# Attention weights of the last 16 keys of each query block: four small transposes and products, and one of each

## The chip, the cores and the metric

The kernel runs on one NeuronCore of a Trainium2 chip. The metric is the device time of one execution in microseconds (us); lower is better. The times given are medians of several runs, with the range.

## The reference

A decoder block on 16 learned meta tokens and 512 tokens (528 rows, model width 1024), all in float32:

```python
h = layer_norm(concat(meta, x))
q_d, k_d, v_d, g_d, q_s, k_s, v_s, g_s, m_d, m_s = split(h @ w_in)        # 1024 x 10240
# 8 differential heads: two softmax maps with a distance bias, their difference times V
a = softmax(q0 @ k0.T / 8 - slope * dist) - lam * softmax(q1 @ k1.T / 8 - slope * dist)
y_d = rms_norm(a @ v) * (1 - lam_init)
# 16 stick-breaking heads
a = exp(log_sigmoid(z) + suffix_sum(log_sigmoid(-z)))      # z = q @ k.T / 8, strictly earlier keys
y_s = a @ v
y = (sigmoid(m_d) * ((y_d * silu(g_d)) @ w_br_d) + sigmoid(m_s) * ((y_s * silu(g_s)) @ w_br_s)) @ w_out
out = layer_norm(2 ** 0.25 * h + y)[16:]
```

Queries are taken in blocks of 128. The meta tokens stand in front, so block i (0 to 3) of queries sees 16 + 128 (i + 1) keys: 144, 272, 400 and 528. Counted in key tiles of 128, block i has full tiles 0 to i and, in tile i + 1, a *strip* of 16 keys. Row r of the block sees strip key k only where r >= 112 + k, so the strip's weights are zero for all but the last 16 queries of the block.

## The kernel before

The work goes by 16 units: 8 differential heads, then 8 pairs of stick-breaking heads. While a unit's attention runs, the projections of the next units (queries, keys, values, gates) fill TensorE; after the last unit come the branch products, the output product and the last norm. Every float32 product that needs accuracy is made of float32r products: a matrix is rounded to a high part (by ScalarE, a cast) and the rest is its low part (by VectorE, a subtraction), and two or three of the four cross products are summed in PSUM. Some small products run in plain float32.

For each head:

- `d_scores` (L817) or `s_scores` (L897) go through the blocks from 3 down to 0. They write the weights of block i to columns `AOFF[i]` on of a padded tile, `apad0` or `apad1`, queries on the partitions. The pad behind the last key of each block is cleared once at the start (L588).
- `transposed` (L762) turns the weights so that keys stand on the partitions. `full` turns a 128 x 128 tile, `strip` the 128 columns that begin with block i's strip. Three steps, each with one PSUM bank (tag `tp`, two buffers): `part0` turns key tile 0 of four blocks into t0; `part1` turns into t1 the strip of block 0, the strip of block 3, and key tile 1 of blocks 1 to 3; `part2` turns into t2 the strip of block 1, key tile 2 of blocks 2 and 3, the strip of block 2, and key tile 3 of block 3. That is 14 transposes. A strip's transpose uses `turned`, an identity turned by 32 columns, so that the block's last 32 queries come out first; the next full tile overwrites the others. So each key tile j has the 32 queries before its first full block and then its full blocks: 512, 416, 288, 160 and 32 columns for tiles 0 to 4 (`QOFF`, L41).
- `split` (L772) makes the high and low parts of each tile (L775 on ScalarE, L776 on VectorE). In a differential head tile 3 (160 columns) is only copied and stays float32 (L808). Tile 4, 16 keys by 32 queries, gets small casts and a subtraction of its own (L793 to L796).
- `values` (L721) turns the V of the unit at hand, projected one unit earlier: four full tiles into tv, and the last 16 keys into t4 (L730, output of 16 partitions), with high and low parts.
- `d_values` (L856) and `s_values` (L918) accumulate V times weights in one bank `av`. A differential head takes tile 0 three times (L861, L869, L870), tile 3 in float32 (L862), tile 4 with high and low parts stacked on the partitions (L863), and tiles 1 and 2 three times each (L866 to L868). A stick-breaking head takes tile 0 twice (L923, L929), tile 4 once (L924) and tiles 1 to 3 twice each (L927, L928).

What sets the order: `run` (L571) gives each step (a block's scores, a part of the transposes, the value products) a place by an estimated time within the unit, and the parts of the projections advance in between. From the units on, a scheduler with a model of each engine then orders the instructions; up to that point and after the attention part, `keep_order` (L233) fixes the order as written. Each engine runs its queue in order, so an instruction that waits holds up all behind it.

Of the kernel before, what the change touches and what calls it, by code (L numbers as in the profile page):

```python
# [16 lines left out]
P = 128  # L17
# [11 lines left out]
AOFF = [0, 256, 640, 1152]  # L29
AW = 1792  # L30
# [10 lines left out]
QOFF = [0, 96, 224, 352, 480]  # L41
# [4 lines left out]
def hybrid_block_kernel(ctx: ExitStack, tc: tile.TileContext, x, meta, emb_g, emb_b, w_in, b_gate,  # L46
# [224 lines left out]
    idents = const.tile([P, 192], F32, name="idents")  # L271
    ident, turned = idents[:, 32:32 + P], idents[:, :P]
    make_identity(nc, ident)
    g.tensor_copy(idents[:, :32], ident[:, 96:])
# [308 lines left out]
    with tc.tile_pool(name="att", bufs=1) as ap:  # L583
        apads = []
        for n in range(2):
            a = ap.tile([P, AW], F32, name=f"apad{n}")
            for i in range(NB):
                g.memset(a[:, AOFF[i] + NKEY[i]:(AOFF + [AW])[i + 1]], 0.0)  # L588
            apads.append(a)

        tails = {}
        v4d = ap.tile([P, P], F32R, name="v4d")
        v4s = ap.tile([P, 4, 64], F32R, name="v4s")
        for n in ("d", 0, 1):
            tails[n] = (v4d if n == "d" else v4s[:, 2 * n:2 * n + 2].rearrange("p c d -> p (c d)"),
                        ap.tile([P, 32], F32R, name=f"a4{n}"))
        for t in (v4d, v4s, *(tails[n][1] for n in tails)):
            g.memset(t.bitcast(F32), 0.0)
# [122 lines left out]
        def values(unit, kind):  # L721
# [7 lines left out]
            t4 = ptp.tile([P, 512], F32, tag="tp", name="t4")[:M, :P]  # L729
            pe.transpose(t4, vT[:, 512:528], ident)  # L730
            if kind == "d":
# [4 lines left out]
                vf = ap.tile([P, P], F32, tag="vf", name="vf")  # L736
                s.copy(vf, tvv[:, 3, :])
                v4 = tails["d"][0]
                s.copy(v4[:M], t4)
                s.copy(v4[32:32 + M], t4)  # L740
                v.tensor_tensor(v4[64:64 + M], t4, v4[:M].bitcast(F32), op=ALU.subtract)
                unit["V"] = V, vf
            else:

                V = V.rearrange("p (j c d) -> p j c d", j=4, c=4)
                for h, l, src in ((V[:, :, 0:4:3], V[:, :, 1:3], tvv.rearrange("p j (c d) -> p j c d", c=2)),
                                  (v4s[:M, 0:4:3], v4s[:M, 1:3], t4.rearrange("p (c d) -> p c d", c=2))):
                    s.copy(h, src)
                    v.tensor_tensor(l, src, h.bitcast(F32), op=ALU.subtract)
                s.copy(v4s[32:32 + M, 0:4:3], t4.rearrange("p (c d) -> p c d", c=2))  # L750
# [11 lines left out]
        def transposed(ta, a, head):  # L762
# [3 lines left out]

            def strip(t, o, i, rot=True):

                c = AOFF[i] + (i + 1) * P
                pe.transpose(t[:, ds(o if rot else o - 96, P)], a[:, c:c + P], turned if rot else ident)  # L770
# [8 lines left out]
            def part0():  # L779
                t0 = ptp.tile([P, 512], F32, tag="tp", name="t0")  # L780
                for i in range(4):
                    full(t0, i * P, i, 0)
                ta[0] = split(t0, 512, 0)

            def part1():
                t1 = ptp.tile([P, 512], F32, tag="tp", name="t1")
                strip(t1, 0, 0)
                strip(t1, 416, 3, rot=False)
                for i in range(1, 4):
                    full(t1, 32 + (i - 1) * P, i, 1)  # L790
                ta[1] = split(t1, 416, 1)
                a4, t4 = tails[head][1], t1[:M, 416:448]
                s.copy(a4[:M], t4)  # L793
                if head == "d":
                    s.copy(a4[64:64 + M], t4)
                v.tensor_tensor(a4[32:32 + M], t4, a4[:M].bitcast(F32), op=ALU.subtract)  # L796
# [462 lines left out]
```

## Time and profile before

| | |
|---|---|
| time, median of 3 runs | 721.54 us (720.97 to 724.15) |
| span of the profiled execution, first to last instruction | 717.8 us |
| granted TensorE clock, mean over the span | 0.996 |
| instructions | 13500 |
| matmul records on TensorE | 4558 |

No total time is given for the profiled execution apart from its span; the median of the runs is 3.7 us above the span, for what lies around it.

In the rows below, PE is TensorE's matmuls, PEld its weight loads, DVE VectorE, ACT ScalarE, POOL GpSimd, SP the DMA-issuing engine. `L765` is a line of the kernel; `t<-idents,apad` says what is written and read, by tile name without buffer number; `128*128 128x416` is a matmul's array size and its moving operand. `x4` is a count. What stands in brackets is the engine's idle time before an instruction and who ended it. Matmul records overlap, so a record's length is longer than the step from its start to the next start. A plain float32 product leaves two records.

### The profile page before, as it was taken

Reading aid. Unit: us, or ns where it says so; the run is one execution under the profiler, and the core shown is the slowest. Engines: PE = TensorE matmul, PEld = TensorE weight load, DVE = VectorE, ACT = ScalarE, POOL = GpSimd, SP = SyncE. Lnnn points to the kernel's source line nnn. Section 1 sums busy time; section 2 is a strip of 40 time slices with the busy share of each in tenths; the row PEclk is TensorE's granted clock in tenths of the full one; section 3 lists DMA queues with packets and bytes.
Section 4 is the critical chain, followed back from the end, with each engine's and each line's share of the span. In section 5 each row is a group of like instructions: output and inputs, shape, how many; then the busy total and the mean of one; then the engine's idle time right before and its main releaser. Section 6 shows DMA issues by size and latency. Waiting matters only on the chain.

```text
span 717.8 us, 13500 instructions
## 1 busy us (share of the span) xinstructions
PE 705.1 (98%) x4558; PEld 643.9 (90%) x4558; DVE 572.1 (80%) x1255; ACT 433.2 (60%) x1041; POOL 126.4 (18%) x151
## 2 busy tenths in 40 slices
PE   8999999999999999999999999999999999999994
PEld 8999999989999888998989899988888998999884
DVE  6887888878696767989887898976396888688887
ACT  5775676757576677867757586765265456555300
POOL 3213210212212111212123020000012102130002
PEclk9999999999999999999999999999999999999998
DMA  9358864779889885998897976556449847696902
GB/s 292 90 168 162 178 143 107 174 164 190 214 173 198 194 179 153 178 230 178 215 215 168 211 157 192 146 151 192 158 121 184 152 120 180 136 187 185 322 17 102
DMA packets 182183, 123.38 MB, mean 172 GB/s; under 512 B 9009, under 2 KB 165074, under 8 KB 182114
## 3 DMA queue, kind: packets, MB, share of 16 engines
q1 hardware_dynamic: 148130, 102.32, 49.5%
q0 software_dynamic: 33664, 19.14, 21.3%
q10 hardware_dynamic: 320, 1.06, 0.4%
q8 instruction: 36, 0.59, 0.3%
q14 instruction: 33, 0.27, 0.1%
HBM read 91.96 MB, written 9.44 MB: 141 GB/s over the span
## 4 chain that ended last, share of the span: by engine, by line
PE 86%; DVE 5%; DMA 3%; ACT 3%; issue 1%; POOL 1%; SPq 0%; ACTq 0%; DVEq 0%; POOLq 0%
PE q L693 15%; PE ps L496 12%; PE ps L497 12%; PE ps L498 12%; PE q L1066 10%; PE ps L512 7%; PE sc L759 6%; PE t L765 4%; PE t L770 1%; DMA lgb<-in_ln_b_dram 1%; PE av L927 1%; PE bank L387 1%; PE tv L726 1%; PE av L928 1%; DVE hr L1216 1%
## 5 line engine op out<-in xcount | busy, mean ns | idle before, releaser
L188 DVE TENSOR_TENSOR wl<-raw,wh 128x512 fp32r<-128x512 f32 x169 | 114.7, 686 | 45.4 <-ACT wh L183 39.1
L497 PE MATMUL ps<-hTl,wh 128*128 128x512 f32 x368 | 144.7, 393 | 0.0
L498 PE MATMUL ps<-hTh,wl 128*128 128x512 f32 x368 | 144.5, 393 | 0.0
L496 PE MATMUL ps<-hTh,wh 128*128 128x512 f32 x368 | 144.5, 393 | 0.0
L183 ACT CAST wh<-raw 128x512 fp32r<-128x512 f32 x169 | 103.0, 620 | 35.3 <-PE ps L497 23.0
L498 PEld LDWEIGHTS ps<-hTh,wl 128*128 128x128 f32 x368 | 69.2, 188 | 13.6
L496 PEld LDWEIGHTS ps<-hTh,wh 128*128 128x128 f32 x368 | 69.2, 188 | 13.3 <-DVE kvt L710 0.3
L497 PEld LDWEIGHTS ps<-hTl,wh 128*128 128x128 f32 x368 | 69.2, 188 | 13.1
L146 POOL DMA_DIRECT2D rawk<-in_w_in_dram x44 | 60.9, 1669 | 95.8 <-DMA rawk<-in_w_in_dram 40.8
L759 PE MATMUL sc<-k,A 128*128 128x264 f32 (+3 forms) x320 | 67.8, 300 | 0.2 <-POOL k L605 0.2
L1066 PE MATMUL q<-gh,wh 128*128 128x256 f32 x224 | 63.5, 283 | 0.2 <-ACT t L1075 0.2
L1066 PE MATMUL q<-gh,wl 128*128 128x256 f32 x224 | 63.4, 283 | 0.0
L1066 PE MATMUL q<-gl,wh 128*128 128x256 f32 x224 | 63.4, 283 | 0.0
L776 DVE TENSOR_TENSOR al<-t,ah 128x512 fp32r<-128x512 f32 (+2 forms) x88 | 45.5, 524 | 20.6 <-ACT ah L775 17.8
L913 DVE TENSOR_TENSOR_SCAN e<-e,diag 128x528 f32<-128x528 f32 (+1 forms) x64 | 53.8, 845 | 7.1 <-ACT e L907 7.1
L775 ACT CAST ah<-t 128x288 fp32r<-128x288 f32 (+3 forms) x88 | 39.8, 462 | 30.1 <-PE t L765 19.8
L759 PEld LDWEIGHTS sc<-k,A 128*128 128x128 f32 x320 | 50.6, 189 | 3.2 <-POOL k L605 0.4
L693 PE MATMUL q<-tS,wh 128*128 128x264 f32 x176 | 50.8, 290 | 0.0
L693 PE MATMUL q<-tl,wh 128*128 128x264 f32 x176 | 50.3, 286 | 0.0
L693 PE MATMUL q<-tS,wl 128*128 128x264 f32 x176 | 50.0, 285 | 0.0
L938 POOL DMA_DIRECT2D ys<-half x14 | 11.8, 840 | 197.0 <-ACT ys L937 187.2
L512 PE MATMUL ps<-hTh,wh 128*128 128x264 f32 x160 | 46.1, 288 | 0.0
(290 smaller groups left out, 1870.5 us busy)
## 6 DMA issues: line engine op xcount, KB each, us to landing
raw<-in_w_in_dram SPq DMA_DIRECT2D x141, 256.0 KB, 3.5
rawk<-in_w_in_dram POOLq DMA_DIRECT2D x44, 256.0 KB, 5.9
rawk<-in_w_in_dram SPq DMA_DIRECT2D x33, 256.0 KB, 4.7
k<-ks SPq DMA_DIRECT2D x60, 132.0 KB, 3.2
raw<-in_w_out_dram SPq DMA_DIRECT2D x16, 256.0 KB, 3.3
k<-ks SPq DMA_DIRECT2D x60, 66.0 KB, 3.2
A<-low SPq DMA_DIRECT2D x28, 128.0 KB, 3.9
raw<-in_w_br_diff_dram SPq DMA_DIRECT2D x12, 256.0 KB, 3.1
```

The source lines that it names most:

```text
L146: second[l] = [lambda raw=raw, x=x: g.dma_start(raw, x, accum_op=ALU.add) for x in more]
L183: s.copy(wh, raw)
L188: eng.tensor_tensor(wl, raw, wh.bitcast(F32), op=ALU.subtract)
L496: pe.matmul(ps, wh[:, k % 4, :], hTh[:, k, M:], start=(k == 0), stop=False)
L497: pe.matmul(ps, wh[:, k % 4, :], hTl[:, k, M:], start=False, stop=False)
L498: pe.matmul(ps, wl[:, k % 4, :], hTh[:, k, M:], start=False, stop=(k == KT - 1))
L512: pe.matmul(ps[:, :H2], a[:, k % 4, :], b[:, k, ts(c, H2)], start=(k == 0 and m == 0), stop=(k == KT - 1 and m == 2))
L693: pe.matmul(bank, a[:, k, :], b, start=start and k == 0 and j == 0, stop=k == 3 and j == 2, skip_group_check=not start)
L759: pe.matmul(ps[:, :n], q, K[:, m, k0:k0 + n], start=(m == 0), stop=(m == 1))
L776: v.tensor_tensor(l, t[:, o:o + w], h.bitcast(F32), op=ALU.subtract)
L913: v.tensor_tensor_scan(rev, rev, diag[0][:, L - nk:][:, ::-1], 0.0, ALU.mult, ALU.max)
L1066: pe.matmul(bank, a[:, k, :], b[:, n, k, :], start=start and k == 0 and m == 0, stop=k == 3 and m == 2, skip_group_check=not start)
```

## The change

The strip of 16 keys is no longer part of the key tiles. Key tiles begin at the block's own first query (512, 384, 256 and 128 columns), and tile 3 stays float32 in both kinds of head.

The four strips of a head are handled together. `strips` lets ScalarE copy them, each twice, into a tile `sx` of 128 columns, ordered (block, copy, key). One transpose gives 4 x 2 x 16 partitions by 128 queries. Only its last 32 queries are used: VectorE repeats them four times along the columns and multiplies by a constant mask `own_block`, which leaves each block's own rows in its own 32 columns (`x`). ScalarE and VectorE then make one float32r tile `m` whose first copies hold the high parts and second copies the low parts, with the sign column `sides`. The product of V's strips, arranged in the same 128 rows, with `m` is written to the last 32 queries of each block, four pieces of 32 columns of `av`. V's 16-key strips (key tiles 128 on, 16 keys each) pass through the same `strips` copy and one transpose of 128 columns.

The padding of the weights' tiles and its clearing go, `idents` becomes a plain identity, and the strips of a head have a common step of 544 columns in the padded tile.

```diff
-AOFF = [0, 256, 640, 1152]
-AW = 1792
+AOFF = [0, 416, 832, 1248]
+AW = 1776
+STRIP, SW = P, 544
...
+        v4 = ap.tile([P, 4, 64], F32R, name="v4")
+        v3 = ap.tile([P, 3, 64], F32, name="v3")
+        own_block = ap.tile([P, NB, 32], F32, name="own_block")
+        sides = ap.tile([P, 2], F32, name="sides")
+        g.memset(own_block, 0.0)
+        for i in range(NB):
+            g.memset(own_block[ds(32 * i, 32), i, :], 1.0)
...
 def values
-            t4 = ptp.tile([P, 512], F32, tag="tp", name="t4")[:M, :P]
-            pe.transpose(t4, vT[:, 512:528], ident)
+            t4 = ptp.tile([P, 512], F32, tag="tp", name="t4")[:, :P]
+            pe.transpose(t4, strips(vT[:, P:], P), ident)
...
+        def strips(t, w):
+            o = ap.tile([P, P], F32, tag="sx", name="sx")
+            s.copy(o.rearrange("p (a h r) -> p a h r", a=NB, h=2), bass.AP(t.tensor, t.offset, [t.ap[0], [w, NB], [0, 2], [1, M]]))
+            return o
...
 def part0
+                ta["strips"] = strips(a[:, STRIP:], SW)
...
 def part1
-                strip(t1, 0, 0)
-                strip(t1, 416, 3, rot=False)
+                pe.transpose(t1[:, 384:], ta["strips"], ident)
                 for i in range(1, 4):
-                    full(t1, 32 + (i - 1) * P, i, 1)
-                ta[1] = split(t1, 416, 1)
-                a4, t4 = tails[head][1], t1[:M, 416:448]
-                s.copy(a4[:M], t4)
-                if head == "d":
-                    s.copy(a4[64:64 + M], t4)
-                v.tensor_tensor(a4[32:32 + M], t4, a4[:M].bitcast(F32), op=ALU.subtract)
+                    full(t1, (i - 1) * P, i, 1)
+                x = ap.tile([P, NB, 32], F32, tag="ax", name="ax")
+                v.tensor_tensor(x, t1[:, 480:].unsqueeze(1).to_broadcast([P, NB, 32]), own_block, op=ALU.mult)
+                m = ap.tile([P, NB, 32], F32R, tag="am", name="am")
+                s.activation(m, x, AF.Identity, scale=sides[:, 1:2])
+                ta[1] = split(t1, 384, 1)
+                v.scalar_tensor_tensor(m, x, sides[:, 0:1], m.bitcast(F32), op0=ALU.mult, op1=ALU.subtract)
+                ta["strips"] = m
...
 def part2
-                strip(t2, 0, 1)
                 for i in range(2, 4):
-                    full(t2, 32 + (i - 2) * P, i, 2)
-                strip(t2, 288, 2)
-                full(t2, 320, 3, 3)
-                ta[2] = split(t2, 288, 2)
-                if head == "d":
-                    ta[3] = ap.tile([P, 160], F32, tag="ah3", name="af3")
-                    s.copy(ta[3], t2[:, 288:448])
-                else:
-                    ta[3] = split(t2, 160, 3, 288)
+                    full(t2, (i - 2) * P, i, 2)
+                full(t2, 2 * P, 3, 3)
+                ta[2] = split(t2, 256, 2)
+                ta[3] = ap.tile([P, P], F32, tag="af3", name="af3")
+                s.copy(ta[3], t2[:, 256:384])
...
 def d_values
-            pe.matmul(av[:, QOFF[3]:], vf, ta[3], start=False, stop=False)
-            pe.matmul(av[:, QOFF[4]:], v4, a4, start=False, stop=False)
+            pe.matmul(av[:, 3 * P:], v3[:, 0:2].rearrange("p c d -> p (c d)"), ta[3], start=False, stop=False)
+            ends = av.rearrange("p (i q) -> p i q", i=NB)[:, :, 96:]
+            pe.matmul(ends, h, ta["strips"], start=False, stop=False)
+            pe.matmul(ends, l, ta["strips"], start=False, stop=False)
...
 def s_values
-            pe.matmul(av[:, QOFF[4]:], v4, a4, start=False, stop=False)
-            for j in range(1, 4):
-                o = av[:, QOFF[j]:]
+            pe.matmul(av[:, 3 * P:], v3[:, c:c + 2].rearrange("p c d -> p (c d)"), ta[3], start=False, stop=False)
+            pe.matmul(av.rearrange("p (i q) -> p i q", i=NB)[:, :, 96:],
+                      v4[:, 2 * c:2 * c + 2].rearrange("p c d -> p (c d)"), ta["strips"], start=False, stop=False)
+            for j in range(1, 3):
+                o = av[:, j * P:]
```

Where instructions moved, at three places of the differential heads. TensorE's transposes of a differential head's weights, into t0 and t1 (the two numbered `t`), between the projection's products; before:

```order
L759 MATMUL sc<-k_456,A_1309 128x264 x4
L512 MATMUL ps<-hTh,wh 128x264
L512 MATMUL ps<-hTl,wh 128x264
L765 MATMUL t_1583<-idents,apad_434 128x128 x4
L770 MATMUL t_1595<-idents,apad_434 128x128 x2
L765 MATMUL t_1595<-idents,apad_434 128x128 x3
L512 MATMUL ps<-hTh,wl 128x264
```

and of the change, whose lines are numbered by its own file:

```order
L510 MATMUL ps<-hTl,wh 128x264
L510 MATMUL ps<-hTh,wl 128x264
L766 MATMUL t_1581<-ident,apad_433 128x128 x4
L784 MATMUL t_1593<-ident,sx 128x128
L766 MATMUL t_1593<-ident,apad_433 128x128 x3
L510 MATMUL ps<-hTh,wh 128x264
```

Nine transposes become eight, and the fifth, of `sx`, reads what ScalarE has copied. In the first head TensorE's value products stand as follows before (`af` is tile 3, `a4d` tile 4, `ah` and `al` the high and low parts):

```order
L862 MATMUL av<-af_927,vf 128x160
L863 MATMUL av<-a4d,v4d 128x32
L866 MATMUL av<-ah_907,V 128x416
L867 MATMUL av<-al_908,V 128x416
L868 MATMUL av<-ah_907,V 128x416
L866 MATMUL av<-ah_923,V 128x288
L867 MATMUL av<-al_924,V 128x288
L868 MATMUL av<-ah_923,V 128x288
```

and with the change (`am` is the block-diagonal tile `m`, `v` the tiles `v3` and `v4`):

```order
L854 MATMUL av<-af_920,v_436 128x128
L856 MATMUL av<-am,v_435 128x4x32
L857 MATMUL av<-am,v_435 128x4x32
L860 MATMUL av<-ah_904,V 128x384
L861 MATMUL av<-al_905,V 128x384
L862 MATMUL av<-ah_904,V 128x384
L860 MATMUL av<-ah_916,V 128x256
L861 MATMUL av<-al_917,V 128x256
L862 MATMUL av<-ah_916,V 128x256
```

The place in the row is the same, one product is added and all others are narrower. ScalarE's queue in the same head, from the last softmax of block 0 to tile 1's cast; before:

```order
L846 ACTIVATE e_455,zs<-e_455,mn 128x144
L183 CAST wh<-raw 128x512
L614 ACTIVATE A_968<-ps 128x512
L846 ACTIVATE e_454,zs<-e_454,mn 128x528
L775 CAST ah_894<-t_889 128x512
L775 CAST ah_907<-t_901 128x416
```

and with the change:

```order
L838 ACTIVATE e_447,zs<-e_447,mn 128x144
L183 CAST wh<-raw 128x512
L760 COPY sx<-apad_433 128x128
L183 CAST wh<-raw 128x512
L611 ACTIVATE A_962<-ps 128x512
L838 ACTIVATE e_446,zs<-e_446,mn 128x528
L771 CAST ah_888<-t_883 128x512
L760 COPY sx<-vT 128x128
L790 ACTIVATE am<-ax,sides 128x128
L771 CAST ah_904<-t_895 128x384
```

The weights' strip copy stands behind one weight cast, V's strip copy and the sign pass between the casts of tiles 0 and 1. On VectorE the mask stands ahead of tile 0's subtraction and the combination behind it.

More of the change, by code (lines that the diff above doesn't have):

```diff
@@ L856, in d_values @@
         def d_values(unit, ta):
-            (vh, vl), vf = unit["V"]
-            v4, a4 = tails["d"]
+            vh, vl = unit["V"]
+            h, l = [v4[:, 2 * m:2 * m + 2].rearrange("p c d -> p (c d)") for m in range(2)]
             av = pav.tile([P, 512], F32, tag="av", name="av")
```

54 lines of the change are left out of this document (19 added, 35 removed).

## The prediction

> **What bounds the kernel now.** I read the page first, then the two long stretches by window, then TensorE's own timeline. The page's busy row, and its row on the chain that ended last by engine:
>
> ```profile
> PE 705.1 (98%) x4558; PEld 643.9 (90%) x4558; DVE 572.1 (80%) x1255; ACT 433.2 (60%) x1041; POOL 126.4 (18%) x151
> PE 86%; DVE 5%; DMA 3%; ACT 3%; issue 1%; POOL 1%; SPq 0%; ACTq 0%; DVEq 0%; POOLq 0%
> ```
>
> TensorE is busy nearly always and carries 86% of the chain. The edit lies in the attention part. Busy times there by window (width, then PE, weight loads, VectorE, ScalarE, GpSimd with counts, granted clock, DMA share, GB/s), the first for the eight differential heads, the second for the eight stick-breaking pairs:
>
> ```profile
> 33.00:251.00 218.00, 217.82 (x1492) 203.44 (x1491) 174.50 (x506) 144.68 (x371) 48.51 (x48) 1.00 0.77 173
> 251.00:522.00 271.00, 270.81 (x1697) 243.43 (x1697) 213.30 (x398) 180.97 (x456) 38.53 (x36) 1.00 0.75 181
> ```
>
> In 489 us TensorE has no record running for 0.18 + 0.19 = 0.37 us, at clock 1.00. VectorE is at 80% and 79%, ScalarE at 66% and 67%, DMA at 0.77 and 0.75: all have room on average. So here the time is the sum of what TensorE is given to do.
>
> Records overlap, since one starts before its forerunner has ended; a duration is not what an instruction costs. I go by the distance from start to start. [...]
>
> **Prices of what goes and comes.** First transposes, and their neighbours, in the first head (timeline of TensorE: start, length of the merged records, count):
>
> ```profile
> 61.80 0.60 PE L765 MATMUL t<-idents,apad 128*128 128x128 f32 x4
> 62.24 0.38 PE L770 MATMUL t<-idents,apad 128*128 128x128 f32 x2
> 62.46 0.49 PE L765 MATMUL t<-idents,apad 128*128 128x128 f32 x3
> 62.70 0.37 PE L512 MATMUL ps<-hTh,wl 128*128 128x264 f32 x1
> 62.91 0.29 PE L512 MATMUL ps<-hTh,wh 128*128 128x264 f32 x1
> ```
>
> From 61.80 to 62.91 nine transposes and one 264-column product start. The chain of waits in order of time has long unbroken runs that price that product, the 256-column one and float32:
>
> ```profile
> 12.45 2.62 PE bank L387 x16
> 15.94 3.51 PE bank L387 x24
> 137.53 1.70 PE q L693 x14
> 550.14 40.31 PE q L1066 x336
> ```
>
> 264 columns: 1.70 / 14 = 0.12 us; 256 columns: 40.31 / 336 = 0.12 us. So a transpose costs (1.11 - 0.12) / 9 = **0.11 us**. L387 multiplies in float32, which leaves two records for each product. Its 16 records are eight of 128 and eight of 256 columns, the 24 are the same and eight more of 128: (3.51 - 2.62) / 8 = 0.111 us a record, **0.22 us** for a 128-column float32 product. Now the value products, stick-breaking then differential:
>
> ```profile
> 279.14 0.34 PE L759 MATMUL sc<-k,A 128*128 128x144 f32 x2
> 279.31 0.23 PE L924 MATMUL av<-a,v4s 128*128 128x32 f32 x1
> 279.39 0.43 PE L927 MATMUL av<-ah,V 128*128 128x416 f32 x1
> 279.66 0.35 PE L928 MATMUL av<-al,V 128*128 128x416 f32 x1
> 279.85 0.29 PE L927 MATMUL av<-ah,V 128*128 128x288 f32 x1
> 279.98 0.40 PE L498 MATMUL ps<-hTh,wl 128*128 128x512 f32 x1
> 280.21 0.39 PE L496 MATMUL ps<-hTh,wh 128*128 128x512 f32 x1
> ...
> 281.14 0.24 PE L928 MATMUL av<-al,V 128*128 128x160 f32 x1
> 281.21 0.43 PE L929 MATMUL av<-al,V 128*128 128x512 f32 x1
> 281.48 0.40 PE L496 MATMUL ps<-hTh,wh 128*128 128x512 f32 x1
> ```
>
> ```profile
> 71.55 0.44 PE L862 MATMUL av<-af,vf 128*128 128x160 f32 x2
> 71.71 0.29 PE L863 MATMUL av<-a4d,v4d 128*128 128x32 f32 x1
> 71.85 0.44 PE L866 MATMUL av<-ah,V 128*128 128x416 f32 x1
> 72.12 0.35 PE L867 MATMUL av<-al,V 128*128 128x416 f32 x1
> 72.31 0.35 PE L868 MATMUL av<-ah,V 128*128 128x416 f32 x1
> ```
>
> 416 columns: 279.85 - 279.66 = 0.19. 288: 0.13. 512: 0.23. From 279.14 to 279.66 stand two products of 144, one of 32 and one of 416: (0.52 - 0.19) / 3 = 0.11 each, so 32 columns cost what 144 do. 160 columns with the 512 behind: 0.34 - 0.23 = 0.11. In the differential head 71.55 to 72.31 holds the float32 product of 160, the 32 and two of 416: 0.76 - 0.38 - 0.11 = 0.27 for the float32 one.
>
> **The change on TensorE, counted over the whole order.**
> - Transposes of weights: 336 become 240 of full tiles and 24 of strips: 72 fewer x 0.11 = **-7.9**. The 16 of V's last keys stay 16.
> - Float32r products of 160 columns in the stick-breaking heads: 32 x 0.11 = **-3.5**.
> - Float32 products: 8 x 0.27 go, 24 x 0.22 come: -2.2 + 5.3 = **+3.1**.
> - Strip products: 24 of 32 columns go (24 x 0.11), 32 of 4x32 columns come (two in a differential head, one in the others): -2.6 + 3.5 = **+0.9**.
> - Narrower tiles: 56 products of 416 become 384. 384 has no row; between 264 (0.12) and 416 (0.19) it is about 0.175: 56 x 0.015 = -0.8. 56 of 288 become 256: 56 x 0.01 = -0.6. **-1.4**.
>
> The unknown is the 4x32 product, 128 float32r columns written in four pieces. The nearest rows, 32, 144 and 160 columns, all give 0.11, which I take; 0.22, the float32 price, is the upper end, +3.5 us in all. Below 0.11 I see no row: even 32 columns take that.
>
> V's strip transpose now loads 128 weight columns where it loaded 16:
>
> ```profile
> L730 PEld LDWEIGHTS t<-idents,vT x10: 87/88/88, 44.8 to 454.4; 128*16 128x16 f32 x10
> 73.36 0.27 PE L730 MATMUL t<-idents,vT 128*16 128x128 f32 x1
> 73.39 0.75 PE L759 MATMUL sc<-k,A 128*128 128x272 f32 x4
> 73.97 0.28 PE L512 MATMUL ps<-hTh,wh 128*128 128x264 f32 x1
> ```
>
> 0.61 us hold it and four products of 272 (about 0.12 each): 0.12 already, so I count nothing. [...]
>
> **The start.** Before the first scores GpSimd clears pads and strip tiles, then K; TensorE waits for it once:
>
> ```profile
> 31.07 1.12 POOL L588 MEMSET apad<- 128x112 f32 x8 [13.76 <-DVE nlam L450]
> 33.42 0.39 PE L759 MATMUL sc<-k,A 128*128 128x264 f32 x1 [0.17 <-POOL k L605]
> ```
>
> The eight pad clears go, five clears of the mask and one ramp for the bias (moved ahead of K) come: K is cleared no later. **-0.2**.
>
> **The other engines, and the added waits.** Rows on single pieces of work (views by tile: least / median / most ns; then one row of VectorE's timeline and one of ScalarE's):
>
> ```profile
> L776 DVE TENSOR_TENSOR al<-t,ah x88: 296/570/693, 63.3 to 515.5; 128x512 fp32r<-128x512 f32 x24, 128x416 fp32r<-128x416 f32 x24, 128x288 fp32r<-128x288 f32 x24, 128x160 fp32r<-128x160 f32 x16
> L796 DVE TENSOR_TENSOR a<-t,a x16: 179/180/181, 276.9 to 511.7; 16x32 fp32r<-16x32 f32 x16
> L793 ACT CAST a<-t x16: 157/172/177, 275.4 to 510.8; 16x32 fp32r<-16x32 f32 x16
> L737 ACT COPY vf<-tv x8: 243/256/262, 47.4 to 232.8; 128x128 f32<-128x128 f32 x8
> 58.91 0.37 DVE L853 SCALAR_TENSOR_TENSOR apad<-e,rz,e 128x144 f32<-128x144 f32 x1
> 59.59 0.62 ACT L183 CAST wh<-raw 128x512 fp32r<-128x512 f32 x1 [1.72 <-PE ps L497]
> ```
>
> VectorE gets 24 masks and 24 combinations of 128 columns, at most 0.37 each (the 144-column row): +17.8; it loses 16 x 0.30 and 24 x 0.18: -9.1. At most +9 on 387.8 us busy. ScalarE gets 40 strip copies and 24 sign passes near 0.26: +16.6, and loses 32 casts of 0.17 and 16 of 160 columns (0.30, taken as VectorE's): +6 on 325.7; V's own casts come out even. Both fit into the idle rest, so they count nothing as long as nobody waits.
>
> Three waits are new. (1) ScalarE copies the strips once VectorE has written the last block; behind it on ScalarE stand a weight cast, the query cast and t0's cast. TensorE turns the strips right behind t0's four transposes; behind it stand three transposes and the projection. The last block ends at 58.91 + 0.37 = 59.28, the strip transposes started at 62.24: 2.96 us, in which ScalarE has one weight cast (to 60.21, after a wait for TensorE) ahead of a copy of 0.26. The copy of V's strip waits for nothing late, since V is a unit old. (2) ScalarE's sign pass waits for VectorE's mask, with the 384-column cast queued behind. (3) VectorE's combination waits for the sign pass, with score work queued behind; the strip product needs it microseconds later. From below these cost nothing; from above one cast of 0.62 in each of 24 heads, 14.9 us. Since the cover is 2.96 against 0.26, I take the low end: as much idle time again as TensorE has now, **+0.4**.
>
> **Sum:** -7.9 - 3.5 + 3.1 + 0.9 - 1.4 - 0.2 + 0.4 = **-8.6 us**, from a span of 717.8 to 709.2. The median of the runs is 721.54, 3.7 us above the span for what lies around it, which stays: **712.9 us**.
>
> **The rivals.**
> - *The 4x32 product costs the float32 price*, for its few columns or its four pieces: +3.5, 716.4. The 144- and 160-column rows speak against it; that no row writes in pieces speaks for it. Chance 0.09.
> - *VectorE becomes the bound* among the stick-breaking heads: it stands still for a cast in progress and the sign pass (0.62 + 0.26) in each of 24 heads, 21 us, of which a quarter reaches TensorE through late weights: +5, about 718. Against it: 57.7 us idle in that window. Chance 0.09.
> - *The weights' DMAs set the pace* and the gain stays as idle time: 717 to 719. DMA shares of 0.77 and 0.75 speak against it. Chance 0.04.
> - *Slower:* TensorE waits at the strip transpose for ScalarE's copy, stuck behind a weight cast that itself waits for TensorE (1.72 us in the row above). It decides from 9.0 / 24 = 0.38 us a head, where the gain is gone; at 0.53 it is slower by 0.5%. A wait of 0.62 + 0.26 a head costs 21.1: 733.6. It needs the 2.96 us of cover to vanish. Chance 0.04.
> - *Forecast:* 0.74.
>
> A measurement of this kernel tells some 0.5%, 3.6 us, from no change. Below 717.9 lie the forecast, the first rival and nearly half of the second: 0.87; within 0.5%: 0.09; slower: 0.04. The forecast's own spread is 710.8 (narrow products cheaper, no hand-off lost) to 715; with the 4x32 price it reaches 716.4, and 717.0 leaves about 0.2 out.
>
> **What would show it.** Right: a TensorE row of 280 transposes, nine starts of L766 and L784 still 0.11 us apart, 4x32 products 0.11 from start to start, TensorE idle under 1 us in the attention windows, which get shorter by about 9 us together, and nothing changed after them. Wrong: TensorE rows with ScalarE's strip copy or VectorE's combination as releaser, 4x32 starts 0.22 apart, or VectorE above 90% in the second window.

## The result, and the profile after

The changed kernel takes **716.64 us** (median of 6 runs, 715.86 to 717.36) where the kernel before, run beside it, takes 721.72 (720.97 to 724.15): a ratio of **0.9928 [0.9905, 0.9951]**, or -5.1 us. The forecast was 712.9, with a range of 710.8 to 717.0. The span of the profiled execution went from 717.8 to 714.6 us, -3.2 where the sum said -8.6. The span missed its forecast by 5.4 us and the time by 3.7 only, because the prediction added too much around the span. Its 3.7 us is the median of the kernel before less the span of its profiled execution, and these are two different executions. Where time and span of one execution are both on record, 1.7 to 2.9 us lie between them, and 1.8 in most (2.4 in the profiled run here). With 1.8 the forecast would have been 711.0. Three single executions of 985 to 4008 us, far above all others of their kernels, are left out of the figures below.

The page's busy row and its row on the chain by engine, and two stretches by window (width; busy time and count of PE, weight loads, VectorE, ScalarE, GpSimd; granted clock; DMA share; GB/s), all of the changed kernel:

```profile
PE 698.9 (98%) x4494; PEld 637.0 (89%) x4494; DVE 571.8 (80%) x1265; ACT 439.1 (61%) x1065; POOL 125.9 (18%) x143
PE 83%; DVE 8%; DMA 4%; ACT 3%; issue 1%; POOL 1%; SPq 0%; DVEq 0%; ACTq 0%; POOLq 0%
33.00:251.00 218.00, 217.78 (x1495) 203.65 (x1495) 177.02 (x516) 148.04 (x379) 49.48 (x49) 1.00 0.78 176
251.00:522.00 271.00, 269.33 (x1655) 240.64 (x1653) 213.15 (x404) 185.34 (x474) 37.26 (x34) 1.00 0.74 178
```

TensorE's share of the chain fell from 86 to 83% and VectorE's rose from 5 to 8%. In the first window TensorE idles 0.22 us, as before. In the second it idles 271.00 - 269.33 = 1.67 us where it idled 0.19. The largest waits of TensorE by who ended them (total us, times, longest):

```profile
PE ps L494 <- ACT wh L183: 1.8, 1, 1.8
PE q L690 <- DVE low L612: 0.9, 2, 0.6
```

The first is one single wait, at the end of the attention part. TensorE's timeline there (start, length, line, out<-in; idle time and its releaser in brackets), for the last head's value products and what follows:

```profile
510.10 0.48 PE L916 MATMUL av<-ah,V 128*128 128x512 f32 x1
...
515.91 0.39 PE L917 MATMUL av<-af,v 128*128 128x128 f32 x2
516.05 0.31 PE L918 MATMUL av<-am,v 128*128 128x128 f32 x1
...
516.43 0.34 PE L923 MATMUL av<-al,V 128*128 128x384 f32 x1
...
516.83 0.39 PE L924 MATMUL av<-al,V 128*128 128x512 f32 x1
...
520.96 0.39 PE L496 MATMUL ps<-hTh,wl 128*128 128x512 f32 x1
523.17 0.64 PE L494 MATMUL ps<-hTh,wh 128*128 128x512 f32 x1 [1.82 <-ACT wh L183]
523.61 0.63 PE L495 MATMUL ps<-hTl,wh 128*128 128x512 f32 x1
524.04 0.69 PE L496 MATMUL ps<-hTh,wl 128*128 128x512 f32 x1
```

From 520.96 to 523.17 are 2.21 us where a step takes 0.23: **1.98 us** stand still. After the restart the steps are 0.43 to 0.44 instead of 0.23. The windows say why (same columns as above; the second number is the width, the number behind the five engines is the granted clock):

```profile
523.00:524.00 1.00, 0.83 (x2) 0.41 (x3) 1.00 (x3) 1.00 (x3) 0.00 (x0) 0.68 0.00 0
524.00:525.00 1.00, 1.00 (x4) 0.81 (x4) 0.72 (x2) 1.00 (x4) 0.00 (x0) 0.50 0.02 6
525.00:526.00 1.00, 1.00 (x4) 0.81 (x3) 1.00 (x3) 0.55 (x2) 0.00 (x0) 0.50 0.68 197
526.00:527.00 1.00, 1.00 (x5) 0.76 (x4) 0.93 (x4) 0.00 (x0) 0.00 (x0) 0.61 1.04 312
```

The granted clock is halved behind the wait: 0.32 + 0.50 + 0.50 + 0.39 = **1.7 us** of TensorE's time are lost. Before, no such stretch stands here:

```profile
523.00:530.00 7.00, 7.00 (x32) 5.82 (x31) 6.40 (x13) 4.59 (x8) 0.00 (x0) 1.00 0.23 68
```

What TensorE waits for is a weight cast at the end of a chain that the last value product starts. ScalarE's and VectorE's timelines of the changed kernel, the links of the chain:

```profile
517.32 0.58 ACT L928 COPY half<-av 64x512 f32<-64x512 f32 x1 [5.75 <-PE av L924]
518.70 0.93 ACT L1043 CAST gh<-ydT 128x256 fp32r<-128x256 f32 x2 [0.81 <-DVE ysT L930]
520.98 1.04 ACT L1043 CAST gh<-t 128x1024 fp32r<-128x1024 f32 x1 [1.34 <-DVE t L1040]
521.93 0.68 ACT L565 ACTIVATE td<-ps,cols 128x512 f32<-128x512 f32 x1
522.51 1.12 ACT L183 CAST wh<-raw 128x512 fp32r<-128x512 f32 x2
```

```profile
517.93 0.69 DVE L930 TENSOR_TENSOR ysT<-av,half 64x512 f32<-64x512 f32 x1 [6.66 <-ACT half L928]
```

From the start of the last value product to TensorE's restart: 523.17 - 516.83 = 6.34 us. TensorE has 18 projection products to fill it, 18 x 0.23 = 4.1 us. In the kernel before, TensorE's and ScalarE's timelines have the same chain:

```profile
515.62 0.43 PE L927 MATMUL av<-ah,V 128*128 128x416 f32 x1
...
518.61 0.30 PE L927 MATMUL av<-ah,V 128*128 128x288 f32 x1
...
519.99 0.43 PE L929 MATMUL av<-al,V 128*128 128x512 f32 x1
```

```profile
520.51 0.58 ACT L933 COPY half<-av 64x512 f32<-64x512 f32 x1 [5.07 <-PE av L929]
525.71 1.13 ACT L183 CAST wh<-raw 128x512 fp32r<-128x512 f32 x2
```

There the cast starts 5.72 us behind the last value product, with the changed kernel 5.68: the chain is as long as ever. What changed is the **cover**. TensorE's order shows it: 947 products of the projections and branches stand behind the last value product before, 930 with the change. The first one that needs the cast is the same, so 35 products cover the chain before (8.0 us) and 18 after (4.1 us).

Why the last value product stands further back is seen in the rows above. The kernel before starts tile 1's products at 515.62 and strews the others between projection products. With the change the float32 product of tile 3 (L917) stands right behind tile 0's in the program, and the scheduler puts it, and so all that follow it, 24 projection products behind tile 0's; then seven come in one block. The copy `af` that it reads had ended at 511.57, over 4 us before:

```profile
511.30 0.27 ACT L802 COPY af<-t 128x128 f32<-128x128 f32 x1 [0.49 <-DVE al L772]
```

So on the chip nothing waits at L917; the lateness is in the order.

The rest of the loss is small. TensorE waits twice for VectorE's `low` of a gate (rows below of the timeline; the step of a 512-column product is 0.23, here 440.37 - 439.26 = 1.11, so 0.88 too long):

```profile
439.26 0.48 PE L916 MATMUL av<-ah,V 128*128 128x512 f32 x1
440.37 0.39 PE L690 MATMUL q<-tS,wh 128*128 128x264 f32 x1 [0.63 <-DVE low L612]
```

Counted from the score products ahead of them, so that the transposes between are included, the places near 314 and 440 us cost 0.6 and 1.1 us; before, one at 261 us cost 0.6. Against the sum of -8.6: +2.0 for the wait, +1.7 for the clock, +1.1 for the small waits, +0.2 for the start, where nothing was gained (before, TensorE waited 0.17 us for the cleared K, now 0.2 for ScalarE's `k`): 5.0 us. The span is off by 5.4, or by 5.8 where the +0.4 for hand-offs that the sum already holds is set against these waits; the rest stays open.

### The profile page after: what moved, and what is told of

It is laid out like the page before. It is cut to its first block, busy times and chain, and to the rows that moved or that the text cites. A ratio compares the mean times of both kernels' runs of the same rounds, so it can differ in the third digit from the quotient of the medians.

```text
span 714.6 us, 13390 instructions
## 1 busy us (share of the span) xinstructions
PE 698.9 (98%) x4494; PEld 637.0 (89%) x4494; DVE 571.8 (80%) x1265; ACT 439.1 (61%) x1065; POOL 125.9 (18%) x143
## 4 chain that ended last, share of the span: by engine, by line
PE 83%; DVE 8%; DMA 4%; ACT 3%; issue 1%; POOL 1%; SPq 0%; DVEq 0%; ACTq 0%; POOLq 0%
PE q L690 15%; PE ps L494 11%; PE ps L495 11%; PE ps L496 11%; PE q L1062 10%; PE ps L510 7%; PE sc L754 5%; PE t L766 3%; PE bank L385 1%; PE tv L723 1%; DMA raw<-in_w_in_dram 1%; DMA raw<-in_w_out_dram 1%; DMA lgb<-in_ln_g_dram 1%; DVE hr L1212 1%; DMA xt<-in_x_dram 1%
## 5 line engine op out<-in xcount | busy, mean ns | idle before, releaser
L772 DVE TENSOR_TENSOR al<-t,ah 128x512 fp32r<-128x512 f32 (+2 forms) x72 | 39.7, 552 | 12.5 <-ACT ah L771 8.6
L771 ACT CAST ah<-t 128x512 fp32r<-128x512 f32 (+2 forms) x72 | 34.2, 477 | 21.3 <-PE t L766 21.1
```

Source lines behind the costliest of these rows:

```text
L772: v.tensor_tensor(l, t[:, o:o + w], h.bitcast(F32), op=ALU.subtract)
```

## The experiments

The **theory**: TensorE's work shrank as predicted (-8.8), and what is missing was lost by the place of tile 3's product: late value products, a chain without cover, a wait, a halved clock. The **rivals**: some product or transpose is dearer than predicted; the new hand-offs on ScalarE and VectorE cost the time; the late cast alone is at fault, wherever the products stand; the profile's wait is an accident. The kernels ran in three sets, each on a chip of its own with the kernel before beside it.

### First set (kernel before: 719.92 us)

**Tile 3 moved behind tiles 1 and 2, all else as changed.**

```diff
 def s_values
             pe.matmul(av, V[c][:, 0, :], ta[0][0], start=True, stop=False)
-            pe.matmul(av[:, 3 * P:], v3[:, c:c + 2].rearrange("p c d -> p (c d)"), ta[3], start=False, stop=False)
...
                 pe.matmul(o, V[c][:, j, :], ta[j][1], start=False, stop=False)
+            pe.matmul(av[:, 3 * P:], v3[:, c:c + 2].rearrange("p c d -> p (c d)"), ta[3], start=False, stop=False)
             pe.matmul(av, V[c][:, 0, :], ta[0][1], start=False, stop=True)
```

> The changed kernel with one line moved: in the stick-breaking heads the float32 product of key tile 3 stands behind the products of tiles 1 and 2 instead of right behind tile 0. Theory A (tile 3, whose weights are ready last, heads the row, so that all seven value products of the last head come late, ScalarE's weight cast behind them comes late, TensorE waits 1.98 us at 523.17 and its clock then falls to half for 3.4 us, 1.9 us more lost): 26 more projection products stand behind the last value product, 44 x 0.23 = 10 us of work against a chain of 6.1 us, so no wait, no half clock, span 714.6 - 3.9 = 710.7 us, time near 712.8. Rival B (the loss at the end comes from the new hand-offs for the strips, which this kernel keeps): span stays at 714.6, time 716.6.

Measured: **711.55 us** (710.62 to 711.69), ratio 0.9868 [0.9848, 0.9889]. 956 products stand behind the last value product; the wait at the end and the halved clock are gone (granted clock 1.00 from 520 to 530 us). That is 5.1 us less than the changed kernel's 716.64 and 3.7 less than its 715.26 in the second set, by one line moved, with the same instructions. These three ran on different chips; against the kernel before beside each, they are -8.4, -5.1 and -4.6 us.

**The gap filled.** Eight float32 products that nothing uses stand ahead of the product that waits; the order and the cast stay late.

```diff
+        if (c, j) == (0, 6):
+            idle = ptp.tile([P, 512], F32, tag="tp", name="idle")[:, :P]
+            for n in range(8):
+                pe.matmul(idle, ident, ident, start=True, stop=True)
         yield from proj_tok(res, "m" + "ds"[c], j)
```

> The changed kernel with eight float32 products of 128 columns without use (0.22 us each, 1.8 us in all) put in TensorE's queue just ahead of the product that waits at 523.17. If the half clock comes from TensorE standing idle there, the wait is filled, the clock stays at 1.00 and the span is 714.6 - 1.9 = 712.7 us. If the half clock comes from something else (a fixed time in the run, the work before it), the clock still falls near 523 and the span stays at 714.6 or grows by up to 0.2.

Measured: 714.97 us (713.84 to 715.8), ratio 0.9917 [0.9899, 0.9935]. Its TensorE rows:

```profile
521.47 1.95 PE L565 MATMUL idle<-ident 128*128 128x128 f32 x16
523.45 0.50 PE L494 MATMUL ps<-hTh,wh 128*128 128x512 f32 x1
...
524.55 0.40 PE L494 MATMUL ps<-hTh,wh 128*128 128x512 f32 x1
524.78 0.39 PE L495 MATMUL ps<-hTl,wh 128*128 128x512 f32 x1
```

The useful products restart as late as ever (523.45), yet the steps are back at 0.22 to 0.23 after three of 0.33 to 0.43, where the first profile has 0.43 to 0.44 at half clock; the span is 713.2, near the 712.7 expected. That fits a clock that is halved by TensorE's standing still, but does not show it: in the second set the unaltered kernel has an execution without the halved clock too, with a span of 712.6.

**The kernel before with tile 3 first.**

```diff
 def s_values
-            pe.matmul(av[:, QOFF[4]:], v4, a4, start=False, stop=False)
-            for j in range(1, 4):
+            for j in (3, 4, 1, 2):
                 o = av[:, QOFF[j]:]
+                if j == 4:
+                    pe.matmul(o, v4, a4, start=False, stop=False)
+                    continue
```

> The kernel before with the value products of the stick-breaking heads in another order alone: key tile 3 (two float32r products of 160 columns) right behind tile 0, then tile 4, 1 and 2. No strip is handled differently. Theory A: 14 fewer projection products stand behind the last value product, 21 x 0.23 = 4.8 us of cover against the chain of 6.1 us: TensorE waits about 1.3 us near 526, and if that is enough for the half clock, 1.9 us more: span 717.8 + 1.3 to 3.2 = 719.1 to 721.0. Rival B: span stays at 717.8.

Measured: 723.76 us (723.17 to 726.45), ratio 1.005 [1.0033, 1.0068]: the kernel before gets slower with another order alone. 933 products stand behind, 21 of them ahead of the cast, and TensorE waits for it:

```profile
531.63 0.50 PE L496 MATMUL ps<-hTh,wh 128*128 128x512 f32 x1 [1.16 <-ACT wh L183]
```

From start to start that wait is 1.32 us, as expected (1.3), and behind it the steps are back at 0.22 to 0.24 us after three of 0.34 to 0.43. The span of 721.4 is above the 719.1 to 721.0 expected: TensorE also waited 1.4 us for a transfer of K, of which more below. So 1.3 of the 3.8 us are shown to come from the late value products.

**Tile 3 of the stick-breaking heads as two float32r products, behind tiles 1 and 2** (the core; V's and the weights' tile 3 are split like the others):

```diff
 def s_values
-            pe.matmul(av[:, 3 * P:], v3[:, c:c + 2].rearrange("p c d -> p (c d)"), ta[3], start=False, stop=False)
...
-            for j in range(1, 3):
+            for j in range(1, 4):
```

> The changed kernel with one part undone: in the stick-breaking heads key tile 3 is split into high and low parts again and multiplied in two float32r products of 128 columns, last but one, instead of one float32 product behind tile 0. Two products of 0.11 against one of 0.22: TensorE's sum the same. VectorE gets 16 subtractions of about 0.27 more. Theory A: 23 products x 0.23 = 5.2 us stand behind the last value product against 6.1 us of chain, so a wait of about 0.9 us instead of 1.98: span 713.5 if the clock still falls to half, 711.6 if it does not. Rival B: 714.6. If the float32 product is dearer than measured, the span falls by more.

Measured: 715.1 us (714.28 to 716.05), ratio 0.992 [0.9903, 0.9938]: 3.6 us worse than the float32 product in the same place. By the prices above one float32 product of 128 columns costs what two float32r products do (0.22), so the price is not the likely reason. The order costs a part: 935 products behind, 23 ahead of the cast, a wait of 0.84 us (0.9 expected):

```profile
523.35 0.50 PE L494 MATMUL ps<-hTh,wh 128*128 128x512 f32 x1 [0.68 <-ACT wh L183]
```

Here too tile 3 stands behind tiles 1 and 2 in the program, and the last value product comes late all the same; why, no run shows. So a place late in the program is not always enough.

In all four profiles of this set TensorE also waited 0.2 to 1.7 us, near 341 us (347 in the kernel before), for the transfer of K, which neither first profile shows; 1.7 us of this kernel's span and 0.9 of the first one's are that. Of the 3.3 us between the two spans (713.2 and 709.9) about 0.8 us is in none of the waits of 0.2 us and more.

### Second set (kernel before: 719.9 us)

**The changed kernel, and the kernel before, unaltered.**

> The changed kernel unaltered, beside the others on one chip. Theory (the last value product comes too late, TensorE then waits for ScalarE's weight cast, and the clock is halved after it): time 715.5 to 717 us, a wait of 1.5 to 2.1 us near 523 us that ends with the cast wh, then 3.4 us at granted clock 0.5. Rival (the loss of the first profile was an accident of that execution): no such wait, time at or below 713.

> The kernel before unaltered. It is to show whether the waits of 0.2 to 1.6 us of TensorE for the transfer of K near 341 us, seen in all four kernels of the first set and in neither first profile, belong to the chip: if so, this profile has one too, of 0.2 to 1.6 us; if they come from those edits, TensorE waits for no transfer near 341 to 347 us here. Time 719.5 to 721.5 us; no wait over 0.7 us and no halved clock behind 510 us.

Measured: 715.26 us (714.41 to 716.97), ratio 0.993 [0.9903, 0.9958], and 721.61 (718.93 to 723.75). The changed kernel waits 1.82 us for the cast at 523.04, as in the first profile: no accident. But in this execution the granted clock stays 1.00 behind it, and the span is 712.6:

```profile
523.04 0.50 PE L494 MATMUL ps<-hTh,wh 128*128 128x512 f32 x1 [1.82 <-ACT wh L183]
524.00:525.00 1.00, 1.00 (x5) 0.82 (x5) 0.71 (x2) 1.00 (x4) 0.00 (x0) 1.00 0.09 20
```

Its runs fall into two groups: four of 714.4 to 715.5 at a mean clock of 0.995 to 0.996, two of 716.7 and 717.0 at 0.993 and 0.994. All six of the first result are of the second kind by their mean clock (0.993 to 0.994). So the wait of 1.98 us stands in both profiles and the halved clock in one, at a price of about 2 us. The kernel before does not wait for K near 341 us here, and the changed kernel does not either; whether that wait belongs to the first set's chip or to its edits, these two profiles can't tell. The kernel before does have a wait that I had not expected, told of at the end.

**The cast made earlier, value products left late.**

```diff
                     steps.append((10.5 + 6.5 * c, lambda c=c, ta=ta: s_values(unit, c, n, ta)))
+            if last:
+                def one_more():
+                    state["ahead"] += 1
+                    prep(len(split))
+                steps.append((17.5, one_more))
             run(proj, steps)
```

> The changed kernel with its order of value products, but the weight half that TensorE waited for near 523 us is fetched and cast one place earlier, ahead of the last head's value products. Theory (the late value product only hurts through the weight cast behind it on ScalarE): the wait for wh near 523 us and the halved clock go, span 710 to 711.5, time 711.8 to 713.3 us. Rival (TensorE is short of work there, whatever is cast, because the gate's operands come late too): a wait of 1 us or more moves to another instruction between 520 and 530 us, time 714.5 or more.

Measured: 714.54 us (713.57 to 714.85), ratio 0.9913 [0.9884, 0.9942]. The theory in this form is wrong and its rival right: the wait goes from the cast to ScalarE's evacuation of a PSUM bank just ahead of it (TensorE's, then ScalarE's timeline):

```profile
521.90 0.50 PE L494 MATMUL ps<-hTh,wh 128*128 128x512 f32 x1 [1.31 <-ACT td L565]
```

```profile
521.17 0.68 ACT L565 ACTIVATE td<-ps,cols 128x512 f32<-128x512 f32 x1
```

ScalarE's whole queue hangs behind the last value product (it is idle for 5.75 us ahead of the copy of `av`, here as in the first profile); taking one link out shortens the chain from 6.34 to 5.82 us and no more. It is the start of the chain that has to move.

**Strips and tile 3 both behind tiles 1 and 2.**

```diff
 def s_values
-            pe.matmul(av[:, 3 * P:], v3[:, c:c + 2].rearrange("p c d -> p (c d)"), ta[3], start=False, stop=False)
-            pe.matmul(av.rearrange("p (i q) -> p i q", i=NB)[:, :, 96:],
-                      v4[:, 2 * c:2 * c + 2].rearrange("p c d -> p (c d)"), ta["strips"], start=False, stop=False)
...
                 pe.matmul(o, V[c][:, j, :], ta[j][1], start=False, stop=False)
+            pe.matmul(av.rearrange("p (i q) -> p i q", i=NB)[:, :, 96:],
+                      v4[:, 2 * c:2 * c + 2].rearrange("p c d -> p (c d)"), ta["strips"], start=False, stop=False)
+            pe.matmul(av[:, 3 * P:], v3[:, c:c + 2].rearrange("p c d -> p (c d)"), ta[3], start=False, stop=False)
             pe.matmul(av, V[c][:, 0, :], ta[0][1], start=False, stop=True)
```

> The changed kernel with both products that are ready late, the strips' and tile 3's, behind tiles 1 and 2 in the stick-breaking heads. Theory (what is ready last must stand last; tile 3 alone mattered): as with tile 3 alone moved, 711 to 712.3 us, no wait over 0.5 us near 523. Rival (the strip product is ready late as well and holds up tiles 1 and 2): another 0.5 to 1.5 us less, 710 to 711 us.

Measured: 710.37 us (710.0 to 711.2), ratio 0.9859 [0.983, 0.9888]. The kernel ran again in the third set, for a profile.

### Third set (kernel before: 720.19 us)

> The changed kernel with tile 3 alone behind tiles 1 and 2, a second time, on another chip. Theory (the waits for the transfer of K near 341 us belong to the chip of the first set): no such wait, 710.3 to 711.3 us, level with the kernel that has both products last. Rival (they come from the earlier finish of the value products): a wait for that transfer of 0.2 us or more again, 711 to 712 us.

> Both late products behind tiles 1 and 2, again, for a profile: 710 to 711.2 us, span 708.2 to 709.4, no wait over 0.7 us of TensorE between 30 and 650 us and no halved clock. Against the quickest group of runs of the kernel before (span 717.2 to 717.6, no wait behind the attention part) that is 8.4 to 9.2 us less, what the prices of TensorE's products alone give (8.8).

Measured, tile 3 alone behind: 711.33 us (710.61 to 711.62), ratio 0.9871 [0.985, 0.9893], with no wait for the transfer of K among TensorE's waits of 0.2 us and more; from start to start 0.28 us are still lost at that place, where the same kernel lost 0.9 us of idle time on the first set's chip. So the chip or the execution matters for that wait, and whether the order adds to it stays open. Both behind: **710.18 us** (709.9 to 711.0), ratio **0.9858 [0.984, 0.9876]**, the fastest kernel of the study. Its busy row and windows, and its last value products in TensorE's timeline:

```profile
PE 697.0 (98%) x4494; PEld 637.0 (90%) x4494; DVE 571.9 (81%) x1265; ACT 438.3 (62%) x1065; POOL 125.7 (18%) x143
33.00:251.00 218.00, 217.79 (x1495) 203.70 (x1495) 177.03 (x516) 147.97 (x379) 49.33 (x49) 1.00 0.78 176
251.00:513.00 262.00, 261.96 (x1626) 235.13 (x1625) 210.86 (x399) 183.74 (x472) 37.28 (x34) 1.00 0.77 184
```

```profile
504.22 0.47 PE L916 MATMUL av<-ah,V 128*128 128x512 f32 x1
504.53 0.34 PE L919 MATMUL av<-ah,V 128*128 128x384 f32 x1
...
509.00 0.28 PE L919 MATMUL av<-ah,V 128*128 128x256 f32 x1
...
509.95 0.48 PE L924 MATMUL av<-al,V 128*128 128x512 f32 x1
```

The counts of records are those of the changed kernel (4494), the work of VectorE and ScalarE the same within 1 us; the products lie apart again, and TensorE idles 0.04 us in the second window.

**The differential heads too**, tile 3 and strips behind tiles 1 and 2:

```diff
 def d_values
-            pe.matmul(av[:, 3 * P:], v3[:, 0:2].rearrange("p c d -> p (c d)"), ta[3], start=False, stop=False)
...
                 pe.matmul(o, vl[:, j, :], ta[j][0], start=False, stop=False)
+            pe.matmul(av[:, 3 * P:], v3[:, 0:2].rearrange("p c d -> p (c d)"), ta[3], start=False, stop=False)
...
```

> As the kernel with both products last in the stick-breaking heads, with tile 3 and the strips behind tiles 1 and 2 in the differential heads too. Theory (only where TensorE runs short of work does the order matter; in the differential heads nothing waited): no change, 710 to 711.2 us. Rival (readiness matters everywhere): 0.4 us or more less, below 709.8.

Measured: 711.53 us (711.14 to 712.25), ratio 0.9876 [0.9858, 0.9894]: no gain, and 1.35 us more than without it, which neither side had expected. A wait for `low` of a gate is back, one of 0.6 us; where the rest is lost was not followed.

**The strip product four times** in the stick-breaking heads (the strips' weights then count fourfold):

```diff
 def s_values
-            pe.matmul(av.rearrange("p (i q) -> p i q", i=NB)[:, :, 96:],
+            for _ in range(4):
+                pe.matmul(av.rearrange("p (i q) -> p i q", i=NB)[:, :, 96:],
```

> Both products last, and the strip product of the stick-breaking heads issued four times instead of once, so that the strips count fourfold: 48 more products of 4x32 columns. At the price taken in the prediction (0.11 to 0.12 us each): 5.3 to 5.8 us more than without, 715.5 to 717 us. At the float32 price of the rival (0.22): 10.6 us more, 720.5 to 721.8.

Measured: 715.94 us (715.16 to 718.34), ratio 0.9944 [0.9924, 0.9963]. Against 710.18: 5.76 us for 48 products, **0.12 us** each. The rival's float32 price (0.22) is out.

### The waits side by side

"Behind" is the number of products of projections and branches behind the last value product. The cover is how many of them stand between it and the one that waits, the chain the time from the start of the last value product to TensorE's restart. The idle time follows as chain - 0.23 - cover x 0.228:

```
kernel                              behind  cover  chain us  follows  measured
changed                             930     18     6.34      2.0      1.98
before, tile 3 first                933     21     6.33      1.3      1.32
changed, tile 3 in float32r, late   935     23     6.39      0.9      0.84
changed, cast earlier               930     18     5.82      1.5      1.47
before                              947     35     -         none     none
changed, strips and tile 3 late     953     41     -         none     none
changed, tile 3 late                956     44     -         none     none
```

The covers of the last three are counted from the same projection product. Since the chain is measured up to the restart, the column "follows" is bookkeeping and no test. What the table shows is that the chain hardly changes (6.33 to 6.39 us) unless a link is taken out, so that the cover decides: at 23 products and fewer TensorE waits, at 35 and more it does not. Tests were the two forecasts of 1.3 and 0.9 us, made from the cover and a chain of 6.1 us before the runs (1.32 and 0.84 measured).

## Why the prediction was right in sign and off in size

- **TensorE's own work (-7.9 - 3.5 + 3.1 + 0.9 - 1.4 = -8.8): right.** With the order mended, the span goes from 717.8 to 708.1, -9.7, of which 0.6 is the wait at 261 us that the kernel before has, and 0.5 is less idle time ahead of 33 us (1.9 against 2.35 us); -8.6 is left. On one chip, the lowest times are 719.51 and 709.9: -9.6. There are 280 transposes, and four of them and one product of 264 columns start between 436.99 and 437.55: (0.56 - 0.12) / 4 = 0.11 us each, as before. In the profile by tile of the changed kernel:

```profile
L766 PE MATMUL t<-ident,apad x240: 270/272/329, 61.4 to 510.1; 128*128 128x128 f32 x120
L784 PE MATMUL t<-ident,sx x24: 271/272/288, 61.9 to 504.6; 128*128 128x128 f32 x24
L727 PE MATMUL t<-ident,sx x16: 270/271/273, 45.5 to 483.0; 128*128 128x128 f32 x16
```

- **The 4x32 product at 0.11: right** (0.12 measured by repetition; 515.91 to 516.43 holds 0.52 us for it, the float32 product and one of 384 columns, and 0.22 + 0.12 + 0.18 is that). The first rival falls with it. The larger weight load of V's strip transposes cost nothing that shows. The stretch of the first head with this transpose and four products of 272 columns, 0.61 us in the prediction, takes 0.62 here (73.53 - 72.91), though the load itself went from 88 to 141 ns (medians of 10 and 16 records):

```profile
72.91 0.27 PE L727 MATMUL t<-ident,sx 128*128 128x128 f32 x1
...
73.53 0.28 PE L510 MATMUL ps<-hTh,wh 128*128 128x264 f32 x1
```

- **VectorE and ScalarE do not bind: right.** VectorE is at 213.15 / 271 = 79% in the second window, ScalarE at 68%. TensorE has no wait of 0.2 us or more for the strip copy or the combination. In the two windows together VectorE is busy 390.2 us in place of 387.8, where up to +9 was counted, and ScalarE 333.4 in place of 325.7 (+6 counted). The second rival and the slower one fall.
- **The start (-0.2): wrong**, nothing was gained there.
- **What lies around the span (+3.7): wrong, and luck.** It is 1.8 in most executions. The 1.9 us too many hid a third of the miss of 5.4 us in the span, and without them 716.64 would lie above the range as well, which would end at 715.1 in place of 717.0.
- **The hand-offs (+0.4): the step that failed.** I priced the three added waits, and no wait of 0.2 us or more on them shows. I did not price the place of the products. I looked at the value products of the first differential head, found ahead of the prediction "the place in the row is the same", and took that for all heads; in the stick-breaking heads tile 3's product was moved from the end to the front of the row. The prediction also said "nothing changed after them", without asking what starts behind the last value product and how much work covers it. That cost 2.0 us of wait and, in some executions, 1.7 to 2 us of halved clock. In the mended order TensorE idles 0.04 us in the second window, in place of 1.67.

How the scheduler arrives at its place for L917 was not tried; that the order in the program moves it is shown in both kernels, by one line moved in the changed one and by another order of the loop in the one before. The float32r run shows that it is not the order alone.

## What to carry to other kernels

Where an edit changes the order of products that sum into one bank, look at the last one before a change of stage: what starts behind it, how long that chain is, and how many products of independent work cover it. A product that the scheduler places late takes along all that stand behind it in the group, in the last head here the six behind L917. In this kernel the late product at the end of its group saved about 3.5 us in the stick-breaking heads, and the same move in the differential heads, where nothing had waited, cost 1.35: so look for the wait first. A saving in instructions was worth its full price here only with a cover at the end of the stage as long as the chain: the same -8.8 us of TensorE's work shortened the span by 3.2 us with a cover of 18 products (4.1 us) for a chain of 6.34, and by 9.7, of which 1.1 are of other places, with one of 41 (9.3 us).

## What the runs showed of the hardware

The granted clock of TensorE was halved behind a single wait, and not every time. After 1.98 us of idle time it was at 0.5 for 3.4 us in the first profile and not at all in the second, at the same place in the same kernel. The same wait thus goes with a span of 714.6 us in the one and of 712.6 in the other; what decides whether the clock falls, no run shows. Behind the waits of 1.32 us (the kernel before with tile 3 first) and 1.47 us (the cast made earlier) the steps were back at 0.22 to 0.24 us from the fourth product on.

The kernel before has such a place of its own, in the branch products, and not in every execution. Its second profile shows TensorE's wait and the steps behind it (0.21 instead of 0.12 us), and the clock by window:

```profile
658.71 0.52 PE L1066 MATMUL q<-gh,wh 128*128 128x256 f32 x1 [2.57 <-ACT t L1071]
659.03 0.42 PE L1066 MATMUL q<-gl,wh 128*128 128x256 f32 x1
659.24 0.41 PE L1066 MATMUL q<-gh,wl 128*128 128x256 f32 x1
```

```profile
659.00:662.00 3.00, 3.00 (x15) 3.00 (x15) 2.51 (x5) 2.72 (x6) 0.00 (x0) 0.50 0.70 231
```

Of the twelve executions of this set six have a span of 717.2 to 718.9 us and six, this one among them, 720.8 to 722.0. The profile of before that the prediction read has 0.2 us of wait at that place and a span of 717.8. Whether the other five wait there too no profile shows; for this one it accounts for 2.7 us of idle time and about 1.7 of clock, so a single profile of the kernel before had left out a place where TensorE can wait. A median of the kernel before thus depends on how many of its executions are of the longer kind.
